# Softmax over 512 columns: loads and stores put in one order on Sync's DMA queue, and the first chunk loaded in three pieces

## Chip, cores and metric

The kernel runs on one core of a Trainium2 chip. Its time is the device time in microseconds (us) of one execution, given as the median of several runs. A separate execution was recorded by the hardware profiler; spans and durations of single instructions come from that one.

## What is computed

A softmax over the last axis, after division by a temperature of 0.5, in float32:

```python
x = np.random.randn(16, 1024, 512).astype(np.float32)
x_scaled = x / 0.5
exp_x = np.exp(x_scaled - np.max(x_scaled, axis=-1, keepdims=True))
return exp_x / np.sum(exp_x, axis=-1, keepdims=True)
```

That is 16,384 independent rows of 512 numbers: 33.55 MB are read from HBM and 33.55 MB are written back.

## The kernel before, in words

The 16,384 rows are cut into 8 chunks of 2,048 rows. A chunk is a tile of 128 partitions with 16 rows of 512 numbers in each, 4 MB in all, and lies in one piece in HBM. There are six tiles (`BUFS`, L42), all called `xt`. Chunks 0 to 5 have a tile each; chunk 6 takes the tile of chunk 0, and chunk 7 that of chunk 1, so their loads must wait until chunk 0, and chunk 1, have been stored. Everything happens in place in the tile.

The work goes by blocks (L39): chunk 0 is three blocks (rows 0 to 3, 4 to 7 and 8 to 15 of each partition), chunks 1 to 6 are one block each, chunk 7 is two halves. For a block there are these steps:

- `shift` (L70 to L81): VectorE (DVE) takes the negated maximum of each row (L77, one instruction for a block), and doubles it (L81). This is the bias of the exponential.
- `exponentials` (L102 to L117): ScalarE (ACT) takes exp(2x + bias) row by row, one instruction for 512 columns of all partitions, and adds up each row's sum on the way (L108).
- `scale_vector` (L120 to L131): DVE takes the reciprocals of the sums (L125) and multiplies most rows by them (L127).
- `scale_scalar` (L133 to L142): ACT multiplies the last eighth of the rows (L138).
- `store` (L144 to L152): after a chunk's last block, one DMA of 4 MB takes the tile to HBM (L148).

The order of each engine's instructions is written out by hand (`manual_schedule`, L47). The loop (L163 to L172) issues, for block i: the exponentials of block i+1, the two scalings of block i, the shift of block i+2, and the store of block i. Only in chunk 1 are the last two exponentials put behind the store of chunk 0 (`rows`, L157 to L160).

Two hardware queues carry the large transfers. The loads are issued by Sync (SP, L68; queue q1 in the profile) from inside `shift`, but since Sync does nothing else, the loads of chunks 0 to 5 are issued at once, and those of chunks 6 and 7 as soon as their tiles are free. The stores are issued by ACT (L148; queue q10), in the order of ACT's own work. Chunk 0 is loaded in two pieces (L38): rows 0 to 3 (1 MB), and rows 4 to 15 (3 MB). Of chunk 7, the last row of each partition (256 KB) is left out of the large load, and GpSimd (POOL) loads it in two DMAs on a third queue, q0, when ACT is in the middle of chunk 5 (`load_last_row`, L88 to L100). At the end Sync waits for everything that is outstanding (L174).

Below, "load 6" is the load of chunk 6, and "store 6" its store.

Of the kernel before, what the change touches and what calls it, by code (L numbers as in the profile page):

```python
# [1 line left out]

# [4 lines left out]


@with_exitstack
def kernel(  # L10
    ctx: ExitStack,
    tc: tile.TileContext,
    x: bass.AP,
    out: bass.AP,
):
    nc = tc.nc
    fp32 = mybir.dt.float32
    P = nc.NUM_PARTITIONS
    AX = mybir.AxisListType.X
    EXP = mybir.ActivationFunctionType.Exp  # L20
    COPY = mybir.ActivationFunctionType.Copy
    MAX = mybir.AluOpType.max

    D = x.shape[-1]
    xf = x.flatten_outer_dims()
    of = out.flatten_outer_dims()
    N = xf.shape[0]

    G = 16
    C = N // (P * G)
    assert C * P * G == N
    xr = xf.rearrange("(c p g) d -> c p g d", p=P, g=G)
    outr = of.rearrange("(c p g) d -> c p g d", p=P, g=G)
    WHOLE = [(0, G)]
    LOADS = [[(0, 4), (4, G)]] + [WHOLE] * 6 + [[(0, G - 1)]]  # L38
    BLOCKS = [[(0, 4), (4, 8), (8, G)]] + [WHOLE] * 6 + [[(0, 8), (8, G)]]  # L39
    STORES = [WHOLE] * 8  # L40
    BMAX = 16
    BUFS = 6  # L42

    data = ctx.enter_context(tc.tile_pool(name="data", bufs=BUFS))
    stats = ctx.enter_context(tc.tile_pool(name="stats", bufs=6))

    ctx.enter_context(tc.manual_schedule())  # L47


    warm = stats.tile([P, 1], fp32, name="warm", bufs=1)  # L50
    nc.vector.memset(warm, 0.0)  # L51
    nc.scalar.activation(out=warm, in_=warm, func=EXP)  # L52

    chunks = {}
    blocks = [(c, lo, hi) for c in range(C) for lo, hi in BLOCKS[c]]
    n = len(blocks)
    biases, sums, recips = {}, {}, {}

    finished = []

    def load(c):
        if c < BUFS:
            chunks[c] = data.tile([P, G, D], fp32, name="xt")
        else:
            chunks[c] = chunks[c - BUFS]
        xt = chunks[c]
        for lo, hi in LOADS[c]:
            part = nc.sync.dma_start(out=xt[:, lo:hi, :], in_=xr[c][:, lo:hi, :])  # L68
            finished.append(part.ins.name)

    def shift(i):
        c, lo, hi = blocks[i]
        if c not in chunks:
            load(c)
        b = hi - lo
        negmax = stats.tile([P, BMAX], fp32, name="negmax")
        nc.vector.tensor_reduce(  # L77
            negmax[:, 0:b], chunks[c][:, lo:hi, :], axis=AX, op=MAX, negate=True
        )
        biases[i] = stats.tile([P, BMAX], fp32, name="bias")  # L80
        nc.vector.tensor_scalar_mul(biases[i][:, 0:b], negmax[:, 0:b], 2.0)  # L81

    def load_last_row(signal):  # L88
        seen = stats.tile([P, 1], fp32, name="seen", bufs=1)
        copied = nc.gpsimd.tensor_copy(out=seen, in_=signal)  # L90
        finished.append(copied.ins.name)
        c = C - 1
        halves = "p (h d) -> p h d"
        to = chunks[c - BUFS][:, G - 1, :].rearrange(halves, h=2)
        of_ = xr[c][:, G - 1, :].rearrange(halves, h=2)
        for p0, p1 in ((P - 2, P), (0, P - 2)):
            part = nc.gpsimd.dma_start(  # L97
                out=to[p0:p1], in_=of_[p0:p1], max_dma_last_dim=2 * D
            )
            finished.append(part.ins.name)  # L100

    def exponentials(i, rows):  # L102
        c, lo, hi = blocks[i]
        if i not in sums:
            sums[i] = stats.tile([P, BMAX], fp32, name="sums")
        for g in rows:
            row = chunks[c][:, lo + g, :]
            nc.scalar.activation(  # L108
                out=row,
                in_=row,  # L110
                func=EXP,
                bias=biases[i][:, g : g + 1],
                scale=2.0,
                accum_out=sums[i][:, g : g + 1],
            )
            if c == BUFS - 1 and g == 10:
                load_last_row(sums[i][:, g : g + 1])  # L117


    def scale_vector(i):  # L120
        c, lo, hi = blocks[i]
        b = hi - lo
        k = b - b // 8
        recips[i] = stats.tile([P, BMAX], fp32, name="recip")
        nc.vector.reciprocal(recips[i][:, 0:b], sums[i][:, 0:b])  # L125
        rows = chunks[c][:, lo : lo + k, :]
        last = nc.vector.tensor_mul(  # L127
            rows, rows, recips[i][:, 0:k].unsqueeze(2).broadcast_to((P, k, D))
        )
        if i == n - 1:  # L130
            finished.append(last.ins.name)  # L131

    def scale_scalar(i):  # L133
        c, lo, hi = blocks[i]
        b = hi - lo
        for g in range(b - b // 8, b):
            row = chunks[c][:, lo + g, :]
            last = nc.scalar.activation(  # L138
                out=row, in_=row, func=COPY, scale=recips[i][:, g : g + 1]
            )  # L140
            if i == n - 1:
                finished.append(last.ins.name)  # L142

    def store(i):  # L144
        c, _, end = blocks[i]
        for lo, hi in STORES[c]:
            if hi == end:
                part = nc.scalar.dma_start(  # L148
                    out=outr[c][:, lo:hi, :], in_=chunks[c][:, lo:hi, :]
                )  # L150
                if c < C - 1:
                    finished.append(part.ins.name)  # L152

    shift(0)
    shift(1)

    def rows(i):  # L157
        c, lo, hi = blocks[i]
        cut = hi - lo - (2 if c == 1 else 0)
        return range(cut), range(cut, hi - lo)  # L160

    exponentials(0, rows(0)[0])
    for i in range(n):  # L163
        if i + 1 < n:
            exponentials(i + 1, rows(i + 1)[0])
        scale_vector(i)
        scale_scalar(i)
        if i + 2 < n:
            shift(i + 2)
        store(i)  # L170
        if i + 1 < n:
            exponentials(i + 1, rows(i + 1)[1])  # L172

    seen = nc.sync.nop()  # L174
    info = mybir.DependencyInfo(
        mybir.DependencyClass.Sync, mybir.DependencyReason.DATA
    )
    for name in finished:
        tc.add_manual_dep(seen.ins, name, info, reason="leaves one wait for the end")


# [1 line left out]
_INS = ['x']  # L183
_OUTS = [((16, 1024, 512), 'float32')]


# [23 lines left out]
```

## Time and profile before

| | |
|---|---|
| median of 3 runs | 161.76 us (161.74 to 162.32) |
| span of the profiled execution, first to last instruction | 160.5 us |
| median less that span | 1.3 us |
| DVE busy | 134.6 us, 84% of the span |
| ACT busy | 102.2 us, 64% |
| DMA, mean over the span | 418 GB/s |
| packets of the loads' queue q1, share of the 16 DMA engines' span | 49.3% |
| packets of the stores' queue q10 | 48.4% |

The profile's busy times belong to engines. DMA traffic has its own rows: how busy the 16 DMA engines were on average, how many GB/s they moved, and for each queue what share of the 16 engines' span its packets took. A DMA is listed by the line that issued it, with the time from its issue to its landing, which is when the engines that wait for it are told. The profile's own words for a large transfer are `xt<-in_x_dram` (a load) and `out_dram<-xt` (a store). Places on the time axis are microseconds from the span's start.

### The profile page before, as it was taken

What the parts mean: (1) busy time and instruction counts of PE and PEld (TensorE: products, weight loads), DVE (VectorE), ACT (ScalarE), POOL (GpSimd) and SP (SyncE); (2) the same over time, 40 slices, a digit from 0 to 9 for tenths busy, and PEclk for the clock granted to TensorE, in tenths of its full rate; (3) what the DMA queues carried; (4) which work ended last, traced back from release to release, by engine and by line L of the source; (5) the groups of instructions that cost most, each with busy time, mean ns of one, the idle gap of its engine ahead of it and who ended that gap; (6) DMA issues with size and microseconds to landing.
All of it is one profiled execution on the core that took longest, in us unless ns stands there. A gap on an engine that the chain in (4) does not pass through costs nothing.

```text
span 160.5 us, 411 instructions
## 1 busy us (share of the span) xinstructions
DVE 134.6 (84%) x45; ACT 102.2 (64%) x273; POOL 1.9 (1%) x7
## 2 busy tenths in 40 slices
DVE  0607999999999999999999999999999999957000
ACT  3071549069989963998199909991899891790000
POOL 0000000000000000000000000030000000000000
DMA  5999999999989999999999999989999999999994
GB/s 184 470 408 498 400 392 457 457 392 402 506 269 425 490 392 400 506 400 392 490 425 392 474 434 392 490 383 483 422 450 400 400 465 441 392 457 449 400 441 204
DMA packets 2578, 67.13 MB, mean 418 GB/s; under 512 B 328, under 2 KB 328, under 8 KB 400
## 3 DMA queue, kind: packets, MB, share of 16 engines
q1 hardware_dynamic: 1296, 33.29, 49.3%
q10 hardware_dynamic: 1152, 33.55, 48.4%
q0 software_dynamic: 128, 0.26, 0.4%
q14 instruction: 2, 0.02, 0.0%
HBM read 33.55 MB, written 33.55 MB: 418 GB/s over the span
## 4 chain that ended last, share of the span: by engine, by line
DVE 75%; DMA 7%; issue 5%; ACT 3%; SPq 0%
DVE negmax L77 42%; DVE xt L127 31%; DMA xt<-in_x_dram 7%; ACT xt L108 3%; DVE bias L81 1%; DVE recip L125 1%; SPq L68 0%
## 5 line engine op out<-in xcount | busy, mean ns | idle before, releaser
L108 ACT ACTIVATE xt<-xt,bias 128x512 f32<-128x512 f32 x128 | 90.4, 708 | 41.5 <-DVE bias L81 40.6
L77 DVE TENSOR_REDUCE negmax<-xt 128x16 f32<-128x8192 f32 (+2 forms) x11 | 69.9, 6352 | 9.4 <-DMA xt<-in_x_dram 9.4
L127 DVE TENSOR_TENSOR xt<-xt,recip 128x7168 f32<-128x7168 f32 (+2 forms) x11 | 62.0, 5637 | 0.4
L108 ACT ACTIVATION_READ_ACCUMULATOR xt<-xt,bias 128x1 f32 x128 | 23.9, 187 | 0.0
L138 ACT ACTIVATE xt<-xt,recip 128x512 f32<-128x512 f32 x15 | 9.9, 706 | 0.0
L125 DVE RECIPROCAL recip<-sums 128x16 f32<-128x16 f32 (+2 forms) x11 | 2.4, 218 | 1.8 <-ACT xt L108 1.8
L81 DVE TENSOR_SCALAR bias<-negmax 128x16 f32<-128x16 f32 (+2 forms) x11 | 1.9, 173 | 0.4
L52 ACT ACT_TABLE_LOAD x1 | 1.3, 1283 | 0.7 <-PEq L194 0.7
L97 POOL DMA_DIRECT2D xt<-in_x_dram x2 | 1.5, 741 | 0.5 <-issue 0.5
L90 POOL COPY seen<-sums 128x1 f32<-128x1 f32 x1 | 0.2, 184 | 103.6 <-ACT xt L108 103.6
L51 DVE MEMSET warm<- 128x1 f32 x1 | 0.1, 59 | 0.8 <-PEq L194 0.8
L52 ACT ACTIVATE warm<-warm 128x1 f32<-128x1 f32 x1 | 0.2, 202 | 0.0
L194 POOL MEMSET const-float32-0.0<- 128x1 f32 x1 | 0.1, 93 | 0.2 <-issue 0.2
L194 POOL MEMSET const-bfloat16-1.0<- 128x1 bf16 x1 | 0.1, 95 | 0.0
L194 POOL MEMSET const-uint8-127<- 128x1 uint8 x1 | 0.1, 95 | 0.0
L194 POOL MEMSET const-float32-1.0<- 128x1 f32 x1 | 0.1, 93 | 0.0
## 6 DMA issues: line engine op xcount, KB each, us to landing
out_dram<-xt ACTq DMA_DIRECT2D x8, 4096.0 KB, 23.1
xt<-in_x_dram SPq DMA_DIRECT2D x6, 4096.0 KB, 34.8
xt<-in_x_dram SPq DMA_DIRECT2D x1, 3840.0 KB, 27.8
xt<-in_x_dram SPq DMA_DIRECT2D x1, 3072.0 KB, 11.6
xt<-in_x_dram SPq DMA_DIRECT2D x1, 1024.0 KB, 4.8
xt<-in_x_dram POOLq DMA_DIRECT2D x1, 252.0 KB, 15.4
xt<-in_x_dram POOLq DMA_DIRECT2D x1, 4.0 KB, 9.1
```

What stands on the lines that cost most here:

```text
L51: nc.vector.memset(warm, 0.0)
L52: nc.scalar.activation(out=warm, in_=warm, func=EXP)
L77: nc.vector.tensor_reduce(negmax[:, 0:b], chunks[c][:, lo:hi, :], axis=AX, op=MAX, negate=True)
L81: nc.vector.tensor_scalar_mul(biases[i][:, 0:b], negmax[:, 0:b], 2.0)
L90: copied = nc.gpsimd.tensor_copy(out=seen, in_=signal)
L97: part = nc.gpsimd.dma_start(out=to[p0:p1], in_=of_[p0:p1], max_dma_last_dim=2 * D)
L108: nc.scalar.activation(out=row, in_=row, func=EXP, bias=biases[i][:, g : g + 1], scale=2.0, accum_out=sums[i][:, g : g + 1],)
L125: nc.vector.reciprocal(recips[i][:, 0:b], sums[i][:, 0:b])
L127: last = nc.vector.tensor_mul(rows, rows, recips[i][:, 0:k].unsqueeze(2).broadcast_to((P, k, D)))
L138: last = nc.scalar.activation(out=row, in_=row, func=COPY, scale=recips[i][:, g : g + 1])
L194: nc = _bacc.Bacc("TRN2", target_bir_lowering=False, num_devices=1)
```

## The change

Four things change together. All stores are issued by Sync, on the queue of the loads. All loads of chunks 0 to 5 are issued before anything else; then the program's order on Sync is: store 0, store 1, load 6, store 2, load 7, store 3, and then stores 4 to 7. Chunk 0 is loaded in three pieces of 1, 1 and 2 MB, one for each of its blocks. And the two exponentials of chunk 1 that stood behind the store of chunk 0 on ACT go back to the others, so that all 16 stand ahead of the last scaling of chunk 0. Instructions on DVE, ACT and POOL are otherwise the same, in the same order; the eight DMA issues leave ACT. GpSimd's load of the last row stays as it was.

```diff
-    LOADS = [[(0, 4), (4, G)]] + [WHOLE] * 6 + [[(0, G - 1)]]
+    LOADS = [[(0, 4), (4, 8), (8, G)]] + [WHOLE] * 6 + [[(0, G - 1)]]
...
     def shift(i):
         c, lo, hi = blocks[i]
-        if c not in chunks:
-            load(c)
         b = hi - lo
...
             if hi == end:
-                part = nc.scalar.dma_start(
+                part = nc.sync.dma_start(
                     out=outr[c][:, lo:hi, :], in_=chunks[c][:, lo:hi, :]
                 )
...
+    for c in range(BUFS):
+        load(c)
+
+    def rows(i):
+        c, lo, hi = blocks[i]
+        return range(hi - lo)
+
     shift(0)
     shift(1)
-
-    def rows(i):
-        c, lo, hi = blocks[i]
-        cut = hi - lo - (2 if c == 1 else 0)
-        return range(cut), range(cut, hi - lo)
-
-    exponentials(0, rows(0)[0])
+    exponentials(0, rows(0))
     for i in range(n):
         if i + 1 < n:
-            exponentials(i + 1, rows(i + 1)[0])
+            exponentials(i + 1, rows(i + 1))
         scale_vector(i)
         scale_scalar(i)
         if i + 2 < n:
             shift(i + 2)
         store(i)
-        if i + 1 < n:
-            exponentials(i + 1, rows(i + 1)[1])
+        c, _, hi = blocks[i]
+        if hi == G and c >= 1 and c - 1 + BUFS < C:
+            load(c - 1 + BUFS)
```

## Prediction

> **What bounds the kernel now.** I read the page first, for who is busy; then the DMA rates by stretches of time; then the landing of single transfers; then the timeline of DVE. On the page, no engine fills the span, but the DMA queues nearly do.
>
> ```profile
> span 160.5 us, 411 instructions
> ...
> DVE 134.6 (84%) x45; ACT 102.2 (64%) x273; POOL 1.9 (1%) x7
> ...
> q1 hardware_dynamic: 1296, 33.29, 49.3%
> q10 hardware_dynamic: 1152, 33.55, 48.4%
> ```
>
> Loads (q1) and stores (q10) together took 97.7% of the 16 DMA engines' span, so the DMA engines have almost no idle time. The next question is whether they are slower in some stretch. Columns: the stretch, its length, DVE, ACT and POOL busy, the clock, the DMA share, GB/s.
>
> ```profile
> 2.00:44.00 42.00, 33.45 (x15) 22.35 (x63) 0.00 (x0) 1.00 1.01 432
> 44.00:46.00 2.00, 2.00 (x1) 1.55 (x5) 0.00 (x0) 1.00 0.78 311
> 46.00:48.00 2.00, 1.93 (x4) 1.73 (x6) 0.00 (x0) 1.00 1.09 262
> 48.00:50.00 2.00, 2.00 (x1) 2.00 (x7) 0.00 (x0) 1.00 1.07 459
> 50.00:110.00 60.00, 59.79 (x14) 46.75 (x126) 1.66 (x3) 1.00 1.01 434
> ```
>
> Loads alone (2 to 44 us) move 432 GB/s; loads and stores in turn (50 to 110) 434: the same ceiling, and no loss from alternating between the two directions. The only slow place is 44 to 48, just behind the first store's issue at 44.10. It counts as busy, so the busy share hides it; the rate shows it. The DMA view of 40 to 52 us has:
>
> ```profile
> DMA packets 160, 4.72 MB, mean 393 GB/s; under 512 B 16, under 2 KB 16, under 8 KB 16
> ```
>
> At 432 GB/s those 12 us would have moved 5.18 MB. The stretch lost 12 x (1 - 393/432) = **1.08 us**, once.
>
> For the stores alone I take the landings of the last four, each from the DMA view narrowed to its issue (at 108.81, 125.43, 133.00 and 147.48):
>
> ```profile
> out_dram<-xt ACTq DMA_DIRECT2D x1, 4096.0 KB, 21.7
> ...
> out_dram<-xt ACTq DMA_DIRECT2D x1, 4096.0 KB, 14.8
> ...
> out_dram<-xt ACTq DMA_DIRECT2D x1, 4096.0 KB, 17.0
> ...
> out_dram<-xt ACTq DMA_DIRECT2D x1, 4096.0 KB, 12.2
> ```
>
> They land at 130.5, 140.2, 150.0 and 159.7: 9.73 us apart. Loads do the same: the second piece of chunk 0 lands at 12.8 (1.16 + 11.6), load 1 at 22.5 (1.64 + 20.9), 9.7 apart. So one 4 MB transfer costs 9.73 us in either direction. From 12.8 to 159.7 there are 15 chunks' worth (loads 1 to 7, stores 0 to 7): 15 x 9.73 = 146.0 of the 146.9 us that passed. The excess, 0.9 us, is the hole again, found a second way.
>
> DVE is the second bound, nearly as tight:
>
> ```profile
> 5.52 2.29 DVE L77 TENSOR_REDUCE negmax<-xt 128x4 f32<-128x2048 f32 x1 [4.65 <-DMA xt<-in_x_dram]
> ...
> 12.80 2.29 DVE L77 TENSOR_REDUCE negmax<-xt 128x4 f32<-128x2048 f32 x1 [4.79 <-DMA xt<-in_x_dram]
> ...
> 24.55 8.68 DVE L77 TENSOR_REDUCE negmax<-xt 128x16 f32<-128x8192 f32 x1
> ...
> 147.48 0.34 ACTq L148 DMA_DIRECT2D out_dram<-xt  x1
> ```
>
> It waits twice for a load at the start and then works without a break until 143.3, which sets the last store's issue at 147.48. But that store did not start then: store 6 landed only at 150.0, and store 7 landed 9.7 us later, as close as stores ever do. The last store queued for DMA, not for DVE. The profile's chain of waits, which follows DVE, doesn't show this.
>
> **The change part by part.** My sum is made on the profiled execution: last landing 159.7, 0.8 us from there to the end of the span, and 161.76 - 160.51 = 1.25 us between span and median.
>
> *Three pieces for chunk 0.* The first lands at 0.74 + 4.8 = 5.5 as before; the second, 1.05 MB at 432 GB/s, 2.4 us later at 7.9; the third at 12.8, as the same bytes did before. DVE's second maximum starts at 8.0 in place of 12.8. That is 4.8 us, but not all is kept. Maximum and bias end at 10.5; the reciprocal waits for ACT's four exponentials (8.05 to 10.98); the multiplication (2.29) ends at 13.5; the third maximum (4.41) and bias at 18.1; reciprocal and second multiplication at 20.6. Then chunk 1 is wanted, and it lands at 22.5. Before, DVE came to it at 24.55. So 2.0 us are kept, and from there every DVE step is 2.0 earlier: chunk 2's load lands two spacings after 12.8, at 32.3, and is wanted at 35.4; later loads have more slack. The last store is ready at 147.5 - 2.0 = 145.5. The extra DMA costs its issue, some 0.4 us on Sync, hidden by the transfers ahead of it. Were DVE the bound this would be worth 2.0; with DMA as the bound it is worth nothing by itself, but it is what keeps the last store from being late (below).
>
> *Stores leave ACT.* Eight issues of 0.34 us, all but a few where ACT waited for DVE anyway (40.6 us idle on the bias): 0. The two moved exponentials likewise: chunk 1's 16 exponentials run from 31.4 to 42.7, and DVE asks for their sums at 44.1.
>
> *One order on one queue.* Loads 0 to 5 now run without a store between: load 5 lands at 12.8 + 5 x 9.73 = 61.5 (before, 3.83 + 73.0 = 76.8). Then in the order of the queue, each landing 9.73 later: store 0 71.2, store 1 80.9, load 6 90.7, store 2 100.4, load 7 (15 of 16 rows) 109.5, and stores 3 to 7, with the 0.6 us of GpSimd's row among them, at 119.9, 129.6, 139.3, 149.1, 158.8. Is each issued in time? Ready times are the issue times before, less 2.0: store 0 at 43, store 1 57, store 2 74, store 3 90, store 4 107, store 5 123, store 6 131, store 7 145.5. Sync goes in order: load 6 waits for store 0's landing (71.2), with store 2 queued behind it; load 7 waits for store 1's (80.9), with store 3 behind it. Each time another 4 MB are still under way, so the queue doesn't run dry. Load 6 is wanted by DVE at 102, load 7 at 118: 11 and 9 us of slack. The tightest is store 7: ready at 145.5, the queue empty at 149.1 less the tail of a landing, some 148.4.
>
> *The hole.* The trace shows no store on a queue that only loads used, so its fate has bounds. Upper gain: all of it goes, 1.08. Below: it stays, 0, or comes at each of the five turns between loads and stores, -4.3 net. What speaks for its going: it falls where a second large queue starts beside one that is running; the first q10 packet is just behind it. After it 60 us of alternating go by without another. I take 1.08.
>
> Sum: 159.7 - 1.1 = 158.6 for the last landing (158.8 by the spacings), 159.4 span, 160.7 time.
>
> Rules of the Trainium skill, weighed. The row: store landings are 9.73 apart on one queue, so nothing is held up at the end of a store by another behind it. "Perfetto Trace Analysis" (DMA Instruction — HWDGE (DVE, Sync)) says that the last descriptor of a DMA waits for its write to be confirmed, with a long delay when the target is HBM. No run here shows a load behind a store on one queue; with the some 2 us that "DMA: Bandwidth & Descriptors" (Anatomy of one DMA — SWDGE (gpsimd) path) gives for this receipt, two loads behind stores would make 164.7, an estimate. And the same page (Issuing engines are not separate DMA queues) says that issuing from several engines saves only the time of issuing; by that, the hole isn't due to the second queue and the time stays at 161.7.
>
> **Rivals.** *The hole stays* (0.30). It comes with the first store, whoever issues it, or store 7 starts as late as store 0 did. For: it follows the first store; store 0 was issued at 44.10 and the rates recover only after 48, some 4 us, where the first load took 1.0 from issue (0.74) to traffic. With 4.3 for store 7: 145.5 + 4.3 + 9.7 + 0.5 landing + 0.8 + 1.25 = 162.0. With the hole unchanged: 161.7. Against: it cost the loads that were running, not the store. This rival is also the case that the change doesn't do what it says: transfers in another order, the same bytes at the same ceiling.
>
> *Each turn costs* (0.20), the slower one. In one queue a turn from loads to stores, or back, must go through the same line of descriptors, where two queues could each run ahead. Price: the start of the load stream lost 0.56 us (1 to 3 us moved 0.30 MB, where 432 GB/s from the first traffic at 1.74 would have moved 0.54). Five turns (load 5 to store 0, store 1 to load 6, load 6 to store 2, store 2 to load 7, load 7 to store 3) make 2.8: 160.7 + 2.8 = 163.5; at 1.08 each 166.1. It decides from (1.1 + 0.8)/5 = 0.38 us a turn. Against: 434 GB/s in 50 to 110, where every DMA engine alternates.
>
> **How the numbers follow.** Forecast 160.7 with 0.50; its own range is 160.3 (the small losses about GpSimd's row, 0.3, go too) to 161.0. The hole stays, 161.4 to 162.1: 0.30. Turns cost: 0.20, from 162.6 on. The range must reach into the last case; 160.2 to 163.5 leaves out some 0.15. A measurement of this kernel can tell about 0.5%, 0.8 us: faster means under 160.95. The chances are those of the three cases: 0.50, 0.30, 0.20.
>
> **What would show it.** The rate around 61 us, where load 5 gives way to store 0, against 432 GB/s: whole, the hole is gone; 393 over 12 us, it stays. The rates at 81, 91, 100 and 110: each dip is a turn's price. Chunk 1's maximum should start at 22.5, the last store be issued near 145.5, and all 4 MB landings follow at 9.73. I am wrong if DVE waits for a load beyond 23 us, if the last store lands over 9.8 us behind the one before it, or if the mean rate falls below 418 GB/s.

## The result, and the profile after

The changed kernel takes 163.44 us (median of 6 runs, 162.17 to 163.85); the kernel before, run beside it, 161.88 (161.74 to 162.32). The ratio, taken over all executions and not of the two medians, is 1.0082, with a 95% interval of 1.0058 to 1.0107: slower, where 160.7 and faster was forecast. The range up to 163.5 just holds it, by way of the rival on the slower side. Of the three signs of being wrong that were named, one came: the mean rate fell to 414 GB/s, below 418.

The first look is at DVE, since there the change was to gain 2.0 us. Timeline of the changed kernel (start, duration, engine, line, operation, and the wait before it):

```profile
span 162.1 us, 412 instructions
...
5.49 2.29 DVE L75 TENSOR_REDUCE negmax<-xt 128x4 f32<-128x2048 f32 x1 [4.62 <-DMA xt<-in_x_dram]
7.96 2.29 DVE L75 TENSOR_REDUCE negmax<-xt 128x4 f32<-128x2048 f32 x1
13.40 4.41 DVE L75 TENSOR_REDUCE negmax<-xt 128x8 f32<-128x4096 f32 x1
22.56 8.69 DVE L75 TENSOR_REDUCE negmax<-xt 128x16 f32<-128x8192 f32 x1 [2.14 <-DMA xt<-in_x_dram]
```

All of this came as worked out: the maxima at 8.0 and 13.4, chunk 1's at 22.6. The last store was issued at 145.50. DVE is 2.0 us ahead, and the kernel is 1.6 us behind all the same. So the loss is in the DMA. Rates of the changed kernel:

```profile
2.00:44.00 42.00, 35.59 (x15) 23.72 (x67) 0.00 (x0) 1.00 1.02 435
...
54.00:66.00 12.00, 11.93 (x4) 7.99 (x23) 0.00 (x0) 1.00 1.00 393
...
88.00:112.00 24.00, 23.86 (x8) 15.98 (x43) 1.67 (x3) 1.00 1.01 434
```

Two things are to be seen. The hole is still there: 393 GB/s over 12 us, the same 1.08 us as before. It has moved from 44 to 48 us to where load 5 gives way to store 0, although store 0 had been issued at 43.5. And the stretch with two more passages from loads to stores (88 to 112) runs at 434 GB/s, without a dent. That speaks against a price for each turn that all DMA engines pay.

The missing time is at the very end. The DMA view of the changed kernel from 157 to 162 us, in 40 slices of 0.125 us:

```profile
DMA  6099699660060000000006000000000000000000
GB/s 262 0 786 786 262 786 524 262 262 0 0 262 0 0 0 0 0 0 0 0 0 262 0 0 0 0 0 0 0 0 0 0 0 0 0 0 0 0 0 0
DMA packets 33, 0.56 MB, mean 111 GB/s; under 512 B 16, under 2 KB 16, under 8 KB 16
```

A packet is entered in the slice where it starts. The crowd of last packets starts until 158.1; one more starts at 158.4, and then a single packet at 159.6. It is one engine of 16, finishing alone. The stretches of one microsecond say the same (DMA share is the last column but one; one packet of 32 KB, 1.21 us on one engine of 16, makes 0.08), first of the changed kernel, then of the kernel before:

```profile
157.00:158.00 1.00, 0.00 (x0) 0.00 (x0) 0.00 (x0) 1.00 1.06 459
158.00:159.00 1.00, 0.00 (x0) 0.00 (x0) 0.00 (x0) 1.00 0.16 66
159.00:160.00 1.00, 0.00 (x0) 0.00 (x0) 0.00 (x0) 1.00 0.08 33
```

```profile
157.00:158.00 1.00, 0.00 (x0) 0.00 (x0) 0.00 (x0) 1.00 1.14 492
158.00:159.00 1.00, 0.00 (x0) 0.00 (x0) 0.00 (x0) 1.00 0.01 0
159.00:160.00 1.00, 0.00 (x0) 0.00 (x0) 0.00 (x0) 1.00 0.00 0
```

Each transfer is split over the 16 DMA engines, and each engine reports its own part's end; a transfer has landed when the last one has reported. The trace keeps these reports. For every transfer I take the last report less the median of the 16, and call it the **lag**. In the changed kernel the median report of store 7 comes at 159.2, where it came at 159.3 before; the last one at 161.2, where it came at 159.7. The second-last of the changed kernel is 0.45 behind the median. One engine is 2.0 us late, and the kernel waits for it. (This is the longest of the six executions, with a span of 162.1; their median span is 161.7, and one has 160.4. So the lag is not as large in each.)

When does this engine fall behind? The lag is 0.20 up to load 2; 0.66 from load 3 on; 1.06 at load 5; 0.78 at store 1; 2.35 at load 6; 2.0 to 2.2 from store 2 on (load 7 itself stands at 2.95, where GpSimd's small loads run as well). Two of the steps stand beside a packet of the queue "instruction", the fetch of 8 KB of instructions by one DMA engine, at 36.4 and at 89.5 us. In the DMA view of 88.5 to 93 us:

```profile
q1 hardware_dynamic: 67, 1.70, 89.2%
q14 instruction: 1, 0.01, 0.4%
```

The trace doesn't name the engine of a packet, but each packet of this stretch starts where another has just ended, so the packets can be strung into 16 rows, one for each engine. Both fetches are then in the row that ends last. The fetch itself took 0.31 us both times. But packets of the queue on that engine took 1.60 (behind the first fetch) and 1.94 and 1.49 us (behind the second), where 1.21 is usual: with the fetch 0.7 and 1.3 us lost. And between the two, at the first passage from loads to stores, this engine lost 1.43 us and the others some 1.0.

### The profile page after: what moved, and what is told of

Its sections match the earlier page's. It is cut to its first block, busy times and chain, and to the rows that moved or that the text cites. A ratio compares the mean times of both kernels' runs of the same rounds, so it can differ in the third digit from the quotient of the medians.

```text
span 162.1 us, 412 instructions
## 1 busy us (share of the span) xinstructions
DVE 134.8 (83%) x45; ACT 101.9 (63%) x273; POOL 1.9 (1%) x7
## 4 chain that ended last, share of the span: by engine, by line
DVE 67%; DMA 13%; issue 5%; ACT 3%; SPq 1%
DVE negmax L75 37%; DVE xt L125 28%; DMA xt<-in_x_dram 13%; ACT xt L106 3%; DVE bias L79 1%; DVE recip L123 1%; SPq L68 1%
## 5 line engine op out<-in xcount | busy, mean ns | idle before, releaser
L106 ACT ACTIVATE xt<-xt,bias 128x512 f32<-128x512 f32 x128 | 90.4, 707 | 39.9 <-DVE bias L79 39.9
```

Of the source, the lines that this page charges most:

```text
L106: nc.scalar.activation(out=row, in_=row, func=EXP, bias=biases[i][:, g : g + 1], scale=2.0, accum_out=sums[i][:, g : g + 1],)
```

## The experiments

All ran on one core beside the kernel before, whose median in the three sets was 161.83, 161.84 and 161.81. The executions' times lie 1.7 to 1.8 us above their spans, in experiments 7 and 9 1.9, in 4 and 6 2.1 to 2.2. A lag is that of one profiled execution of each kernel, mostly the longest; times are medians, and behind each ratio to the kernel before stands its 95% interval.

**1. Two queues again.** In the changed kernel:

```diff
-                part = nc.sync.dma_start(
+                part = nc.scalar.dma_start(
                     out=outr[c][:, lo:hi, :], in_=chunks[c][:, lo:hi, :]
```

> The change with its stores put back on ACT's queue; the three pieces and the order of the loads stay. In the changed kernel the transfers end together on 15 of the 16 DMA engines at some 159.3 us of the span, where they ended in the kernel before, and one engine ends 1.6 us later. Theory A: one queue is what lets this one engine fall behind. Then two queues bring the last landing back to some 159.7 us and the time to that of the kernel before, 161.9, and the 2.0 us that DVE gains by the three pieces show nowhere. Rival B: the three pieces (one more DMA) are what costs; then this kernel stays at some 163.4.

Measured: 162.38 (162.13 to 162.56), ratio to before 1.0029 (1.0018 to 1.0040). 1.06 us of the 1.6 come from putting the stores on the loads' queue. The interval lies clear of the changed kernel's (1.0058 to 1.0107). It doesn't quite return to 161.8: a lag of 1.0 is left.

**2. Two pieces for chunk 0, one queue.** In the changed kernel:

```diff
-    LOADS = [[(0, 4), (4, 8), (8, G)]] + [WHOLE] * 6 + [[(0, G - 1)]]
+    LOADS = [[(0, 4), (4, G)]] + [WHOLE] * 6 + [[(0, G - 1)]]
```

> The changed kernel with chunk 0 loaded in two pieces again: one queue, but one DMA less. Theory A (one queue): it stays at some 163.4, or loses a little more, since DVE is 2.0 us later and store 7 is ready only at 147.5, 0.9 us ahead of the queue's end. Rival B (the third piece costs): 161.9.

Measured: 163.30 (163.06 to 163.78), 1.0093 (1.0079 to 1.0106). In one queue the third piece neither costs nor gains; theory A holds. With two pieces in both kernels, one queue costs 1.5 us (163.30 against 161.83). Its profile ends with a lag of 2.15.

**3. Fewer instructions on ACT.** In the changed kernel, `ones` being a tile set once:

```diff
                 scale=2.0,
-                accum_out=sums[i][:, g : g + 1],
             )
...
-            sums[i] = stats.tile([P, BMAX], fp32, name="sums")
+            sums[i] = ones
```

> The changed kernel without the summing on the way in the exponentials: 128 read-outs of the accumulator fewer on ACT, a constant in place of the sums, so that the output isn't a softmax; the DMAs are the same. Theory A1: the engine that falls behind is the one that also fetches ACT's instructions, 8 KB each, at 36.4 and 89.5 us of the span; the load's landing just behind the second fetch is the first with the lag. With some 160 instead of 290 instructions there is one fetch or none, the lag of one engine is 0.7 us or less, and the time falls by 0.9 to 1.6, to between 161.8 and 162.5. Rival A2: a lag that one queue makes whatever is fetched; then the time stays within 0.5 of 163.4.

Measured: 162.63 (162.24 to 163.75), 1.0062 (1.0037 to 1.0088); 0.8 less than the changed kernel by the medians, a little short of A1's range; the interval overlaps that of the changed kernel. Five of seven executions have spans of 160.5 to 160.9, two have 162.0. The profile is one of these two: one fetch (at 52.2), lag 0.26 before it, 0.95 at load 5, 1.87 at load 6, and 1.98 at the end. So one fetch is enough for the whole lag, but, by the spans, not every time. At 90.5 us, where load 6 gives way to store 2, the late engine lost 0.98 us here with no fetch near, the others at most 0.2.

**4. An early small store.** In the changed kernel, `zeros` being 512 bytes of each partition:

```diff
             finished.append(part.ins.name)
+            if c == 0 and lo == 0:
+                part = nc.sync.dma_start(out=outr[C - 1][:, 0, 0:128], in_=zeros)
+                finished.append(part.ins.name)
```

> The changed kernel with one more store behind the first load: zeros, 512 bytes of each partition (64 KB), into a place that store 7 writes again later. The place of lost rate (1.0 us on all DMA engines, at 44 to 48 us before and at 58 to 61 us after the change, each time just ahead of the first store's packets) comes with the first store, wherever it is. Theory C: it is paid once, by the first store that the DMA engines do; then the stretch 56 to 62 us is back at 432 GB/s and the time 1.0 lower than the changed kernel's, some 162.4, less if the start hides it. Rival D: it belongs to the passage from loads to the first large store, and stays: 163.4 to 163.6.

Measured: 164.06 (163.96 to 164.71), 1.0153 (1.0135 to 1.0171). Theory C falls: a store that all engines did at the start does not take the hole away. The rates of this kernel:

```profile
54.00:66.00 12.00, 11.93 (x4) 7.99 (x23) 0.00 (x0) 1.00 0.97 396
```

396 GB/s against 393. By the reports, the median engine lost 0.5 us between load 4 and store 0, where it lost 0.9 in the changed kernel, so a part of the loss may have gone. The hole belongs to the passage from a long row of loads to the first large store. The time is above D's range too; 0.3 of that lies outside the span (164.06 against 162.0), and its cause is open.

**5. One passage less.** In the changed kernel:

```diff
-        if hi == G and c >= 1 and c - 1 + BUFS < C:
-            load(c - 1 + BUFS)
+        if hi == G and c == 1:
+            load(BUFS)
+            load(BUFS + 1)
```

> The changed kernel with load 7 put right behind load 6, so that Sync's queue goes from loads to stores twice (after load 5, after load 7) and not three times. Theory T: at each passage from loads to stores in one queue a DMA engine that comes to it late loses about 1 us more than the early ones (in the kernel without accumulators the last engine lost 0.98 us at 90.5 and 0.85 at 109.2, the first ones nothing). Then one passage less gives back 0.8 to 1.0: 162.4 to 162.6. Rival F: the lag is made by the fetches of ACT's instructions alone; then 163.1 to 163.4 as in the changed kernel.

Measured: 163.32 (163.24 to 163.95), 1.0101 (1.0088 to 1.0114). Theory T, a fixed price for each passage, is wrong here. The lags of its profile: 0.78 at load 3, 1.45 at load 5, 1.28 at store 1, 2.18 at load 6, 2.3 at the end. With two passages the engine falls as far behind as with three. It is no clean test of a passage, though: the second fetch (89.9 us) fell among loads here and cost its engine 0.6 us, and the last passage 0.8; in the changed kernel a fetch and a passage came together and cost 1.3.

**6. Two passages more.** Loads 6 and 7 and stores 2 and 3 in halves, in turn (`load_part` and `store_part` issue one half each):

```diff
...
-        store(i)
         c, _, hi = blocks[i]
-        if hi == G and c >= 1 and c - 1 + BUFS < C:
-            load(c - 1 + BUFS)
+        if c in (2, 3):
+            load_part(c + 4, 0)
+            store_part(c, 0)
+            load_part(c + 4, 1)
+            store_part(c, 1)
+        else:
+            store(i)
```

> The changed kernel with loads 6 and 7 and stores 2 and 3 each in two halves of 2 MB, taken in turn: five passages from loads to stores in place of three, four DMAs more. Theory T: two more passages cost the late engine 0.8 to 1.0 each: 165.0 to 165.4. Rival F (fetches alone): 163.3 to 163.6.

Measured: 165.19 (164.13 to 165.46), 1.0196 (1.0173 to 1.0220), inside T's range and not quite for T's reason: the median span is 163.0 against 161.7 for the changed kernel, 1.3 us for two passages, and another 0.4 lies outside the span. Passages are not free, then: two more cost 1.3 us, one less gave nothing back. The profile is that of the fastest execution, and no witness for the median.

**7. No fetch at all, one queue.** One exponential for a block, no bias, no sums (`ones` in their place):

```diff
-        for g in rows:
-            row = chunks[c][:, lo + g, :]
...
+                block = chunks[c][:, lo:hi, :]
+                nc.scalar.activation(out=block, in_=block, func=EXP, scale=2.0)
```

> The changed kernel with one exponential for a whole block, without bias and sums (so the output isn't a softmax): some 30 instructions on ACT in place of 290, so that no instruction block is fetched during the work; DVE's work and the DMAs are the same. Theory T with the fetch as what sets one engine behind: no engine is behind the others by more than the 1.2 us of a packet, the lag of 1.6 goes in every run: 162.0 to 162.4, with spans within 0.5 us of each other. If the passages alone make the lag: 163.1 to 163.4, with spans from 160.4 to 162.1 as in the changed kernel.

Measured: 162.69 (162.40 to 163.28), 1.0060 (1.0045 to 1.0075), between the two forecasts. By the medians 0.75 us of the loss are gone without fetches and 0.85 remain. But the interval overlaps that of the changed kernel (1.0058 to 1.0107), and by the ratios it is 0.4 us; experiments 2 and 5, one queue with its fetches, lie clear of it (from 1.0079 and 1.0088 on). So fetches cost something in one queue, some 0.4 to 0.8 us. The profiled execution (the longest, span 161.4) has lags of 0.29 at load 3, 0.37 at load 5, 0.15 at store 1, 0.39 at store 2, and 1.3 from store 3 on. This last step stands where load 7 gives way to store 3 and GpSimd's small loads run; which of the two makes it was not tried.

**8. No fetch, two queues.** The same edit in the kernel before.

> The same edit (one exponential for a block, no bias, no sums; not a softmax) in the kernel before, with its two queues. Both theories: two queues forgive a late engine, so nothing changes beyond 0.3: 161.5 to 161.9. If it falls by as much as the one-queue kernel does, the fetches cost alike in both, and one queue isn't what makes them dear.

Measured: 162.00 (161.73 to 162.44), 1.0010 (1.0000 to 1.0019), 0.1 above the range expected. With two queues the fetches cost nothing that can be seen; with one they cost 0.4 to 0.8. Without fetches, the one-queue form is 0.69 above the two-queue form, 0.5 of it in the span. (Experiment 8 has two pieces for chunk 0, experiment 7 three; how the 0.69 falls to queue and pieces was not tried apart.)

**9. A late engine on purpose, one queue.** In the kernel of experiment 7, behind the pieces of chunk 0:

```diff
+            part = nc.sync.dma_start(
+                out=early[BUFS - 1][0:1].rearrange(flat)[:, 0 : G * D - 1],
+                in_=xr[BUFS - 1][0:1].rearrange(flat)[:, 0 : G * D - 1],
+            )
```

> The one-queue kernel without instruction fetches (one exponential for a block, no bias, no sums; not a softmax), with one DMA engine set behind on purpose: 32 KB of chunk 5 in one partition are loaded once more, as the DMA behind the third piece, on one engine if the transfer isn't split (one packet, 1.21 us). In its profile the last of the 16 engines lands 0.3 us behind the median one up to load 4. Theory T2: one queue enlarges a lag: each passage from loads to stores costs the late engine more than the others, until it is some 2 us behind. Then the 1.2 us become 2.0 or more at the last landing, and the time is 0.7 to 1.5 above that of the same kernel without the extra load (162.69): 163.4 to 164.2. Rival P: a lag is carried to the end and no more: the last landing is 1.2 to 1.6 behind the median one from load 0 on. The second rival is that other engines' spare time takes the lag back, and the time stays at 162.7.

Measured: 164.62 (164.36 to 164.76), 1.0170 (1.0157 to 1.0183): 1.93 us above experiment 7, for one packet of 1.21 us. The extra load did run on one engine, and the lag can be followed: 1.15 from load 1 to load 4, 2.17 at load 5, where the first store comes up, 1.96 at store 1, 2.72 at store 2, 2.62 at the end. The second-last engine ends 0.42 behind the median. Up to load 5 the lag is carried without growing; it grows where loads give way to stores, by 1.0 and by 0.8, and not at the third passage. T2 holds and P falls, though T2's range was too low by 0.4. The end of this kernel, in stretches of 1 us:

```profile
157.00:158.00 1.00, 0.00 (x0) 0.00 (x0) 0.00 (x0) 1.00 1.14 492
158.00:159.00 1.00, 0.00 (x0) 0.00 (x0) 0.00 (x0) 1.00 0.08 33
159.00:160.00 1.00, 0.00 (x0) 0.00 (x0) 0.00 (x0) 1.00 0.08 33
```

It is the picture of the changed kernel, made by hand: one engine with two packets left when the other 15 have started their last.

**10. A late engine on purpose, two queues.** The same extra load in the kernel of experiment 8.

> The same extra 32 KB on one engine in the two-queue kernel without fetches (not a softmax; 162.00 without the extra load). Theory T2: two queues don't enlarge the lag, and the loss of rate at the first store falls less on the late engine than on the others (in the kernel before, the engine that fetched lost 0.77 us there, the others 1.0 to 1.3): 162.2 to 163.0, the last landing 0.4 to 1.2 behind the median one. If it rises by as much as the one-queue kernel does, one queue isn't what enlarges a lag.

Measured: 163.07 (162.38 to 163.59), 1.0074 (1.0051 to 1.0097): 1.07 above experiment 8, against 1.93 in one queue. In the median the same packet costs less than itself here and 1.6 times itself there. But the median lies between two groups: three spans are 160.6 to 161.0, three 161.6 to 161.8, and the profiled one, the longest, has a lag of 1.96 at the end. T2 had 162.2 to 163.0 and a lag of 0.4 to 1.2, and is missed on both. So two queues enlarge a lag in some executions as well; in one queue all five spans were 162.4 to 162.8.

**11. Three pieces alone, in the kernel before.** Only the line `LOADS` of the change.

> The kernel before with chunk 0 loaded in three pieces and nothing else. The two-queue form of the change took 162.38, 0.5 above before, with one engine 1.0 us behind at the end. If the third piece does that (everything on DVE 2.0 us earlier, so the first store meets the loads elsewhere), this kernel is at 162.2 to 162.5; if the two exponentials that were moved ahead of the first store do, it stays at 161.8.

Measured: 162.39 (162.09 to 162.97), 1.0042 (1.0025 to 1.0058), the same as experiment 1. With two queues the third piece costs 0.6 us. Its profiled execution (span 161.1) has a lag of 0.81 at load 3 and 1.58 at the end, where the kernel before has 0.48 and 0.39. In the kernel before, the hole took 0.77 us from the engine that fetches and 1.0 to 1.3 from most others, and so brought it level; with everything 2.0 us earlier it doesn't.

**12. No small loads by GpSimd, in the kernel before.**

```diff
-    LOADS = [[(0, 4), (4, G)]] + [WHOLE] * 6 + [[(0, G - 1)]]
+    LOADS = [[(0, 4), (4, G)]] + [WHOLE] * 7
...
-            if c == BUFS - 1 and g == 10:
-                load_last_row(sums[i][:, g : g + 1])
```

> The kernel before with all 16 rows of chunk 7 loaded by Sync and GpSimd's two small loads gone. DMA is the bound, and around the small loads (110 to 122 us) the profile of before has 423 GB/s where 434 is the rule: 0.3 us. If that is all, 161.5. Against: load 7 lands 0.6 us later, still ahead of DVE's need at 120.5. If it is slower than 161.8, the small loads relieve something that the rates don't show.

Measured: 162.11 (161.99 to 162.25), 1.0020 (1.0011 to 1.0028). It is 0.3 slower and not 0.3 faster; the lag of its profiled execution is 1.07. The gaps that the small loads make on the engines (0.3 us) are not what ends the kernel.

The lags beside one another (from the engines' reports of a transfer's end; with two queues the values between load 4 and store 3 follow the alternation of the queues and are left out):

```
lag, us                        load 3  load 5  store 1  store 2  store 4  store 7   median, us
before (2 queues)               0.48     -       -        -       0.24     0.39      161.8
1  two queues, three pieces     0.57     -       -        -       1.04     0.98      162.4
8  two queues, no fetch         0.28     -       -        -       0.79     0.80      162.0
10 the same, one engine late    1.09     -       -        -       1.94     1.96      163.1
after (1 queue)                 0.66    1.06    0.78     2.03     2.10     2.01      163.4
5  a passage less               0.78    1.45    1.28     2.80     2.32     2.27      163.3
7  no fetch                     0.29    0.37    0.15     0.39     1.26     1.29      162.7
9  the same, one engine late    1.16    2.17    1.96     2.72     2.63     2.62      164.6
```

No kernel here beats the kernel before, and no run points to one that would.

## Why the prediction was wrong, point by point

- *The three pieces.* Right in every time of DVE (8.0, 13.4, 22.56; last store issued at 145.50). "Worth nothing by itself" holds in one queue (experiment 2); in two queues the third piece costs 0.6 us (experiment 11).
- *Stores leave ACT; the two exponentials.* Cost nothing, as said: ACT's idle time before the exponentials is 39.9 us, 41.5 before, and DVE waits for ACT 2.3 us in all, 1.8 before.
- *One order on one queue.* The queue never ran dry. The median engine's reports of stores 3 to 7 come at 120.4, 130.2, 139.9, 149.6 and 159.2, 9.7 apart; 119.9 to 158.8 was forecast.
- *The hole.* This step failed: "I take 1.08" for its going. It stayed, at 393 GB/s over 12 us. It is tied neither to the second queue nor to the issue of the first store, but to the place where the first large store follows the loads, and an early store doesn't do away with it (experiment 4). That alone makes the forecast the rival "the hole stays", 161.7.
- *The term that was missing.* The sum treated the 16 DMA engines as one, at a mean rate. The last landing is that of the last engine. A fetch puts one engine back by some 0.7, one queue makes this some 2.0, and that is the difference: last report less median one 2.0 in place of 0.4. With the hole's 1.08 this is the way from 158.6 to the last landing at 161.2. Putting the stores back on ACT's queue takes 1.06 us off (experiment 1). Experiment 7 gives the fetches' part, some 0.4 to 0.8; experiments 9 and 10 show that one queue enlarges a lag (1.93 for 1.21), two queues in some executions only (1.07 in the median).
- *"Each turn costs"* named the right place, passages from loads to stores, and its 163.5 is what was measured, but by luck, not by its working. There is no 0.56 at each of five turns: rates show none at 88 to 112, and one passage less gives nothing (experiment 5). The price falls on an engine that comes late to a passage (experiment 9: 1.0 and 0.8 us at the first two).
- *The sum's frame.* I added 1.25 us to the span of a profiled execution. The executions measured here stand some 1.77 above their spans, and those of the kernel before have spans of some 160.05; the profiled one, 160.51, was one of the longer ones. This doesn't explain the miss, since the sum is in effect the median of before less 1.1 us. But spans that differ by 0.5 us from one execution to the next are a narrow base for a gain of 1.1.
- *The rule of the Trainium skill on issuing engines* ("DMA: Bandwidth & Descriptors", Issuing engines are not separate DMA queues: several issuing engines save only the time of issuing). The row differs: the same kernel with its stores on ACT's queue is 1.06 us faster (experiment 1), though the changed kernel issued its last store 4 us before its turn (145.5 against 149.6). The measurement decides.
- *The rule on the last descriptor* ("Perfetto Trace Analysis", DMA Instruction — HWDGE (DVE, Sync): it waits for the write to be confirmed, long when the target is HBM). No such wait shows for what is queued behind a store: load 6 landed on the median engine 9.4 us behind store 1 and 19.4 behind store 0.

What stays open: whether it is the single queue or the order of the transfers in it that enlarges the lag. With two queues loads and stores run side by side (load 4 lands at 57.7 in experiment 1, at 52.1 in the changed kernel); with one they run one behind another, and experiment 1 changes both at once. Open too is why a late engine loses about 1 us more than the others where loads give way to stores in one queue, and why it stops at 2 to 3 us. The traces show which packets are longer (the loads just ahead of the store), not what they wait for. Whether the 0.69 us between experiments 7 and 8 belong to the queue alone was not tried.

## What to carry to other kernels

In this kernel, bound by DMA, the end was that of the last of 16 engines, and the mean rates of the stretches before it did not show it. In others like it, look at the last two microseconds of the DMA rows for a share of 0.08, one engine alone, and compare each transfer's last report with its median one. A second queue may be worth more than the time of issuing, because it can keep a late engine from falling further behind, as it did here in the median. And put the span that you reason from beside several executions, not one, before an edit of half a per cent is judged.

## What I had not expected of the hardware

- An instruction fetch of 8 KB took 0.31 us on one DMA engine and delayed the queue on that engine by 0.6 to 0.7 us among loads (experiment 5, changed kernel) and by 1.3 us just ahead of a passage from loads to stores, where a late engine lost 0.98 without one (experiment 3). There were two fetches with ACT's 273 instructions, one with 145 (experiment 3) and none with 28 (experiment 7). Without fetches the two-queue kernel is no faster (162.00 against 161.84).
- One packet of 32 KB on one engine, 1.21 us, cost 1.93 us of kernel time in one queue and, in the median, 1.07 in two.
- The loss of 1.08 us at the first large store behind a row of loads, on all engines (393 GB/s over 12 us), with one queue and with two.
